# An attention kernel: rarer self-waits on ScalarE, a copy of K split over two queues, and the second Q's cast and the V loads held back

## The chip, the cores and the metric

The kernel runs on one core of a Trainium2 chip. The metric is the device time of one execution in microseconds (us), the median of several runs. The profile's span, from the first to the last instruction, is about 1.8 us shorter than that time; all times inside the kernel count from the start of the span.

## The reference

Grouped-query attention, 8 batches, 8 query heads, 2 key/value heads, 1024 tokens, head size 64, all float32 (cut):

```python
scores = scale * np.matmul(q_group, k_group.transpose(0, 1, 3, 2))
scores_max = np.max(scores, axis=-1, keepdims=True)
attn = np.exp(scores - scores_max)
attn = attn / (np.sum(attn, axis=-1, keepdims=True) + 1e-08)
output[:, q_start:q_end, :, :] = np.matmul(attn, v_group)
```

## The kernel before

A planner splits the work into 128 jobs (a batch, a head, one half of its queries) of 8 cells (128 keys x 512 queries), and decides for each cell whether ScalarE takes the exp, two cells to a tile, or VectorE with an approximation made of bits. It also sets the order on every engine. One constant tells it when the second half of the first K is there:

```python
FIRST_TURN, FIRST_LOAD, EACH_LOAD = 3.3, 4.5, 4.2
...
def loaded(j):
    h = j // 2
    if not h:
        return FIRST_TURN * (j % 2)
```

ScalarE writes its exps into a ring of 28 tiles. Every eighth tile waits for a result of ScalarE itself, so that the following ones need not:

```python
exp_ins.append(act.ins)
if n >= P_TILES and n % OBSERVE == 0:          # OBSERVE = 8, P_TILES = 28
    seen = exp_ins[n - P_TILES + OBSERVE - 1]
    tc.add_manual_dep(act.ins, seen.name, SYNC, reason="ring")
```

The first head has no time for DMA transposes: K and Q are loaded in halves, cast, and turned (transposed) by TensorE into PSUM, the memory that TensorE writes; TensorE is kept busy with matmuls on a blank tile (`keep_warm`). Jobs of side 0 use K on partitions 0 to 63 (`lo`), jobs of side 1 use it on 64 to 127 (`hi`). The `hi` half is a copy of the `lo` half by one DMA from GpSimd (cut; the comments are mine):

```python
cast(("q", 0, 1), q[0, 1])            # head 1's Q, GpSimd, issued at once
for two in range(2):
    place_v(0, 0, two)                # V, GpSimd
...
last_score[0] = keep_warm(WARM)       # 30 blank matmuls
...                                   # halves of K and Q: cast, turn, copy from PSUM
nc.scalar.copy(out=qT[(0, 0)][:, : HALF // 2], in_=tq[0][:, : HALF // 2])
turn_k(1, slice(0, NHC), 0)
last_score[0] = keep_warm(4)
put_k(0, 1, slice(0, NHC), 0)
nc.gpsimd.dma_start(out=ksets[0][hi, 0, 1, :], in_=ksets[0][lo, 0, 0, :])
```

The softmax here doesn't subtract the row's maximum and nothing guards it: scores larger than these inputs give would overflow.

## Time and profile before

| | before |
|---|---|
| time, median of 3 runs | 386.83 us (386.65 to 386.90) |
| span of the profiled run | 384.9 us |
| exp tiles on ScalarE | 406, one every 0.917 us |
| first, fourth exp start | 6.47, 9.80 us |
| end of the 403rd exp to end of span | 8.34 us |

From the page of the kernel before, first the busy times (us, share of the span, instructions), then the chain of work that ended last (share by engine):

```profile
PE 368.1 (96%) x5172; PEld 234.5 (61%) x5172; DVE 350.1 (91%) x544; ACT 375.1 (97%) x411; POOL 165.3 (43%) x147
```

```profile
ACT 94%; PE 2%; DMA 1%; issue 1%; DVE 0%; SPq 0%; POOLq 0%
```

TensorE and ScalarE are both nearly always busy. The chain tells which of them sets the end: ScalarE, for 94% of the span. The other 6% of 384.9 us, some 23 us, lie at the start and the end, so a change that doesn't touch ScalarE's rate can only earn there.

### The profile page before, as it was taken

Reading aid. Unit: us, or ns where it says so; the run is one execution under the profiler, and the core shown is the slowest. Engines: PE = TensorE matmul, PEld = TensorE weight load, DVE = VectorE, ACT = ScalarE, POOL = GpSimd, SP = SyncE. Lnnn points to the kernel's source line nnn. Section 1 sums busy time; section 2 is a strip of 40 time slices with the busy share of each in tenths; the row PEclk is TensorE's granted clock in tenths of the full one; section 3 lists DMA queues with packets and bytes.
Section 4 is the critical chain, followed back from the end, with each engine's and each line's share of the span. In section 5 each row is a group of like instructions: output and inputs, shape, how many; then the busy total and the mean of one; then the engine's idle time right before and its main releaser. Section 6 shows DMA issues by size and latency. Waiting matters only on the chain.

```text
span 384.9 us, 12057 instructions
## 1 busy us (share of the span) xinstructions
PE 368.1 (96%) x5172; PEld 234.5 (61%) x5172; DVE 350.1 (91%) x544; ACT 375.1 (97%) x411; POOL 165.3 (43%) x147
## 2 busy tenths in 40 slices
PE   8879999999999999999999999999999999999985
PEld 6425565656666666666666565666566566666654
DVE  4879999999999999999999999999999999999692
ACT  5999999999999999999999999999999999999994
POOL 5394571716246171625535252535445261531410
PEclk9999999999999999999999999999999999999998
DMA  8888979597859769595865949486584756621213
GB/s 137 152 130 141 141 138 173 113 129 148 128 111 134 132 109 141 123 138 85 151 123 126 125 90 169 74 150 113 119 143 109 111 100 113 109 70 29 71 43 83
DMA packets 102422, 45.49 MB, mean 118 GB/s; under 512 B 63776, under 2 KB 100896, under 8 KB 101120
## 3 DMA queue, kind: packets, MB, share of 16 engines
q1 hardware_dynamic: 82096, 31.21, 37.5%
q0 software_dynamic: 19728, 13.25, 29.8%
q8 instruction: 40, 0.66, 0.8%
q10 hardware_dynamic: 544, 0.26, 0.2%
q14 instruction: 14, 0.11, 0.1%
HBM read 25.17 MB, written 27.00 MB: 136 GB/s over the span
## 4 chain that ended last, share of the span: by engine, by line
ACT 94%; PE 2%; DMA 1%; issue 1%; DVE 0%; SPq 0%; POOLq 0%
ACT p_ring L463 94%; PE ops L522 1%; PE aps L452 1%; DMA fk<-in_k_dram 1%; DMA kset<-kset 1%; SPq L389 0%; DVE ost L538 0%; ACT hk L411 0%; DVE kset L382 0%; DVE qT L427 0%; PE aps L373 0%; DVE rec L535 0%; PE ops L419 0%; PE ops L400 0%; POOLq L433 0%
## 5 line engine op out<-in xcount | busy, mean ns | idle before, releaser
L463 ACT ACTIVATE p_ring<-aps 128x1024 bf16<-128x1024 f32 x406 | 372.4, 1100 | 1.2 <-PE aps L452 1.2
L452 PE MATMUL aps<-qT,kset 128*128 128x512 bf16 x812 | 240.6, 378 | 11.4 <-ACT p_ring L463 8.8
L522 PEld LDWEIGHTS <-p_ring 128*128 128x128 bf16 x3248 | 137.5, 97 | 60.4 <-ACT p_ring L463 0.2
L522 PE MATMUL ops<-vset,p_ring 128*128 128x65 bf16 x3248 | 150.8, 194 | 0.1
L477 DVE TENSOR_SCALAR pd<-dps 128x512 uint16<-128x512 f32 x212 | 138.0, 682 | 13.2 <-PE dps L452 12.3
L500 POOL TENSOR_SCALAR y<-z 128x5120 f16<-128x5120 uint16 (+1 forms) x22 | 94.6, 4301 | 82.7 <-DVE rec L535 45.0
L452 PEld LDWEIGHTS <-kset 128*128 128x128 bf16 x1024 | 82.6, 97 | 58.8 <-issue 26.7
L314 POOL DMA_DIRECT2D scr_q<-in_q_dram x63 | 34.7, 551 | 99.0 <-PE aps L452 47.6
L452 PE MATMUL dps<-qT,kset 128*128 128x512 bf16 x212 | 73.4, 378 | 0.0
L511 DVE TENSOR_TENSOR pd<-pd,y 128x5120 uint16<-128x5120 uint16 (+1 forms) x22 | 59.8, 2719 | 0.1
L509 DVE TENSOR_TENSOR y<-z,y 128x5120 f16<-128x5120 uint16 (+1 forms) x22 | 59.8, 2718 | 0.0
L538 DVE TENSOR_TENSOR ost<-ops,rec 128x256 f32<-128x256 f32 x128 | 54.3, 424 | 4.4
L522 PEld LDWEIGHTS <-pd 128*128 128x128 bf16 x848 | 41.3, 98 | 25.6 <-DVE pd L511 3.6
L522 PE MATMUL ops<-vset,pd 128*128 128x65 bf16 x848 | 48.4, 194 | 0.0
L496 DVE TENSOR_SCALAR z<-pd 128x5120 uint16<-128x5120 uint16 (+1 forms) x22 | 31.7, 1443 | 0.6
L535 DVE RECIPROCAL rec<-ops 128x4 f32<-128x4 f32 x128 | 22.5, 176 | 9.8 <-PE ops L522 8.8
L347 POOL DMA_DIRECT2D vset<-in_v_dram x32 | 24.9, 782 | 0.0
L314 POOL DMA_DIRECT2D scr_k<-in_k_dram x15 | 7.8, 521 | 24.1 <-PE aps L452 16.7
L400 PE MATMUL ops<-blank 128*128 128x128 bf16 x40 | 4.4, 286 | 1.1 <-DVE blank L279 1.1
L400 PEld LDWEIGHTS <-blank 128*128 128x128 bf16 x40 | 3.8, 135 | 1.1 <-DVE blank L279 1.1
L354 POOL DMA_DIRECT2D kset<-kset x6 | 3.2, 537 | 0.0
L411 ACT ACT_TABLE_LOAD x1 | 1.3, 1283 | 1.8 <-issue 1.8
(23 smaller groups left out, 8.7 us busy)
## 6 DMA issues: line engine op xcount, KB each, us to landing
out_dram<-ost SPq DMA_DIRECT2D x63, 256.0 KB, 2.9
scr_q<-in_q_dram POOLq DMA_DIRECT2D x63, 128.0 KB, 3.6
kset<-kT SPq DMA_DIRECT2D x60, 64.0 KB, 3.1
vset<-in_v_dram POOLq DMA_DIRECT2D x32, 64.0 KB, 4.0
scr_k<-in_k_dram POOLq DMA_DIRECT2D x15, 128.0 KB, 3.2
qT<-scr_q SPq DMA_TRANSPOSE x63, 4.0
kset<-kset POOLq DMA_DIRECT2D x7, 128.0 KB, 4.0
fq<-in_q_dram ACTq DMA_DIRECT2D x2, 128.0 KB, 3.2
```

The costliest lines, as they stand in the source:

```text
L314: dma = nc.gpsimd.dma_start(out=scr.rearrange("(p f) -> p f", f=1024), in_=src.rearrange("(p s) d -> p (s d)", s=1024 // D),)
L347: nc.gpsimd.dma_start(out=vsets[b % 2][:, g, two * NHC : (two + 1) * NHC, 0:D], in_=v[b, g].rearrange("(c p two) d -> two p c d", p=128, t ...
L452: last_score[0] = nc.tensor.matmul(dst, lhsT=ksets[b % 2][:, h // HPG, side, c * 128 : (c + 1) * 128], rhs=qT[(b, h)], start=True, stop=Tr ...
L463: act = nc.scalar.activation(out=pt[:, 0:m], in_=psum.pop(("A", n))[:, 0:m], func=AF.Exp, scale=scale)
L477: nc.vector.tensor_scalar(out=groups[g][:, slot], in0=psum.pop(cell), scalar1=bits_scale, scalar2=bits_bias, op0=ALU.mult, op1=ALU.add,)
L496: eng.tensor_scalar(out=z, in0=pd, scalar1=0x7F, scalar2=None, op0=ALU.bitwise_and)
L500: eng.tensor_scalar(out=y, in0=z, scalar1=CURVE_A / 128.0, scalar2=CURVE_B, op0=ALU.mult, op1=ALU.add,)
L509: eng.tensor_tensor(out=y, in0=z, in1=y, op=ALU.mult)
L511: eng.tensor_tensor(out=pd, in0=pd, in1=y, op=ALU.add)
L522: nc.tensor.matmul(ops_of[s][:, qs, :], lhsT=p_of[cell][:, qs * 128 : (qs + 1) * 128], rhs=vsets[b % 2][:, h // HPG, c, :], start=opens an ...
L535: nc.vector.reciprocal(out=rec, in_=o[:, :, D])
L538: nc.vector.tensor_tensor(out=stage[(b, h)][:, :, side, :], in0=o[:, :, 0:D], in1=rec.unsqueeze(2).to_broadcast([128, NQS, D]), op=ALU.mult,)
```

## The change

It has three parts, and a constant that goes with them. The self-wait comes once in 26 tiles. The copy of K to `hi` becomes two DMAs: the even keys from ScalarE, as soon as its own copy is done, the odd keys from GpSimd as before. The cast of the second Q and the V loads wait for the 14th blank matmul, to leave the DMA engines to the first K and Q. The planner is told that the copy comes earlier (2.4 instead of 3.3).

```diff
-    FIRST_TURN, FIRST_LOAD, EACH_LOAD = 3.3, 4.5, 4.2
+    FIRST_TURN, FIRST_LOAD, EACH_LOAD = 2.4, 4.5, 4.2
...
-    OBSERVE = 8
+    OBSERVE = 26
...
-        cast(("q", 0, 1), q[0, 1])
-        for two in range(2):
-            place_v(0, 0, two)
...
-        last_score[0] = keep_warm(WARM)
+        last_score[0] = keep_warm(14)
+        cast(("q", 0, 1), q[0, 1])
+        for two in range(2):
+            place_v(0, 0, two)
+        last_score[0] = keep_warm(WARM - 14)
...
+        nc.scalar.dma_start(
+            out=ksets[0][hi, 0, 1, :HALF], in_=ksets[0][lo, 0, 0, :HALF]
+        )
...
-        nc.gpsimd.dma_start(out=ksets[0][hi, 0, 1, :], in_=ksets[0][lo, 0, 0, :])
+        nc.gpsimd.dma_start(
+            out=ksets[0][hi, 0, 1, HALF:], in_=ksets[0][lo, 0, 0, HALF:]
+        )
...
-        if n >= P_TILES and n % OBSERVE == 0:
+        if n >= P_TILES and (n - P_TILES) % OBSERVE == 0:
```

## The prediction

> **What bounds the kernel now.** I read the page first (busy time, groups), then the chain of work in order of time, then the windows view of ScalarE's exp tiles, then the timeline of both ends.
>
> The groups of the page give the work of ScalarE: 406 exp tiles, and next to no idle time ahead of them (1.2 us in all, TensorE being awaited).
>
> ```profile
> L463 ACT ACTIVATE p_ring<-aps 128x1024 bf16<-128x1024 f32 x406 | 372.4, 1100 | 1.2 <-PE aps L452 1.2
> ```
>
> The chain in order of time shows the beginning, and how the first self-wait looks (start us, length us, what):
>
> ```profile
> 1.26 3.09 DMA fk<-in_k_dram
> 4.35 0.02 issue
> 4.37 0.41 ACT hk L411
> ...
> 5.38 0.29 DVE qT L427
> 5.67 0.36 DVE kset L382
> 6.03 0.02 issue
> 6.05 0.02 POOLq L433
> 6.07 0.56 issue
> 6.63 2.48 DMA kset<-kset
> 9.11 0.05 issue
> 9.15 0.62 PE aps L452 x2
> 9.77 0.02 issue
> 9.80 22.80 ACT p_ring L463 x25
> 32.60 0.05 issue
> 32.65 0.87 ACT p_ring L463
> ```
>
> One chain leads from the K load over casts and transposes to the copy of K to the second partition half; this copy lands at 9.11, and the fourth exp starts at 9.80 because of it. From there on the chain is ScalarE alone. The "issue" piece at 32.60 is the first self-wait; after the first five such pieces come, in the same view, one for every 8 tiles, each of 0.04 to 0.09 us. A reader would now multiply: 51 self-waits before (counted in the built program), some 0.05 us each, 2 to 3 us. The windows view says otherwise (stretch, busy, tiles that touch it):
>
> ```profile
> 10.82:32.82 22.00, 22.00 (x25) 1.00 0.83 137
> 33.74:374.75 341.01, 341.01 (x373) 1.00 0.68 117
> ```
>
> I put the edges on ends of tiles (the timeline gives the starts and durations: 9.80 + 1.02 is the end of the fourth exp, 32.65 + 1.09 that of the first one with a self-wait). One tile in each count only reaches over the right edge, so there are 24 and 372 ends. 22.00 / 24 = 0.917 us without a self-wait, 341.01 / 372 = 0.917 us with one in every 8. Tiles last 1.02 to 1.15 us and overlap; a waiting tile starts later and lasts less, its end comes when it would have come. So ScalarE's own rate, 0.917 us a tile, bounds the program from 9.8 to about 377, and the self-waits hide in the overlap.
>
> The timeline of the end (columns: start, length, engine, line, operation):
>
> ```profile
> 376.38 2.95 ACT L463 ACTIVATE p_ring<-aps 128x1024 bf16<-128x1024 f32 x3
> ...
> 377.55 0.59 PE L452 MATMUL aps<-qT,kset 128*128 128x512 bf16 x2
> ...
> 379.82 0.90 PE L522 MATMUL ops<-vset,p_ring 128*128 128x65 bf16 x24
> ```
>
> The last exp ends at 376.38 + 2.95 = 379.33, but TensorE still works on its backlog of output matmuls until 380.72, then come the last division and the store. The last score matmul (377.55) starts as the exp two tiles before the last ends, one free PSUM tile being what it needs.
>
> **What the Trainium skill says.** "ScalarE: Activation LUTs", section "What ACT_TABLE_LOAD costs": 186 ns + 0.833 ns an element for an ACTIVATE with immediate scale, overlapping the next one by some 93 ns; for 1024 elements 1039 - 93 = 946 ns. The trace has tiles of 1100 ns mean every 917 ns, so more overlap than the page states; 917 = 853 + 64 I take from the trace. "Perfetto Trace Analysis", section "Per-instruction lifecycle": for this engine the window starts when execution starts, and the semaphore wait in the wait queue is outside of it. This fits: a wait shows only as a later start, and costs only if the end moves. "DMA: Bandwidth & Descriptors", section "Latency and other measured facts": first byte some 0.6 us on the hardware path, 1 us on the software path. The trace agrees in direction: the software copy of K took 2.48 us from issue to landing (128 KB, a lone transfer), and copies of 64 KB into the same tile from SyncE have medians of 2.3 us (window 60 to 90 us) to 3.1 us (whole page). Same page, "Issuing engines are not separate DMA queues": all share 16 engines, so what ScalarE's issue gains is time of issue, not bandwidth.
>
> **The change part by part.**
>
> *Self-waits.* The built programs have 51 ACTIVATEs with a self-wait before and 15 after. 36 are removed; at the rate above each was worth 0, sum 0. The new wait looks back to the exp 3 before instead of 21 before. That one ended about 3 x 0.917 - 1.10 = 1.65 us before the new tile's start, so it should be satisfied too: cost 0.
>
> *K copy.* Before, exps 1 to 3 start at 6.47 and run 2.85 us, ending at 9.32; the fourth ends at 10.82 instead of 9.32 + 0.92 = 10.24. The stall is 0.58 us, and no more than this can be had. After: the even half is issued by ScalarE when its copy into the tile is done (the program waits for its third result, 5.15 + 0.37 = 5.52, and for an older result of VectorE), so at about 5.6, landing 2.3 to 3.1 us later: 7.9 to 8.7. The planner's constant (3.3 to 2.4) now puts two cells of output matmuls, one VectorE score, then the fourth tile's two scores there. To keep the rate this exp must start by 10.24 - 1.02 = 9.22, so the three scores (3 x 0.216 issue, plus 0.4 for the last to finish) must start by about 8.3. Landing is before that in the lower two thirds of the interval, so I take 0.1 us of the 0.58 as remaining: gain 0.48. The issue takes ScalarE's sequencer some 0.5 us, 5.6 to 6.1, while the first exp waits for scores until 6.43: hidden. The odd half, on GpSimd, waits for VectorE only (done 6.02), as before, is half as large, and must be there at 9.3, when the fifth tile's PSUM comes free: hidden.
>
> *First Q cast and V loads.* They now wait for the 14th warm-up matmul (ends about 2.73) instead of being issued at 1.34. But before, the first packets of the cast only started at 3.61 us, and on each DMA engine behind the last packets of the K and Q loads; these are done at 3.9 (K) and 4.2 (Q). There is little to relieve: I take 0.05 us of gain. On the other side V lands at about 3.4 + 3.4 = 6.8, needed at 8.0, and the cast at about 6.2, with its transpose (3.8 us in the trace) at 10.1, needed at about 10.7: both hidden, the second barely.
>
> *What the plan moves.* 1024 cells were 812 for ScalarE (406 tiles) and 212 for VectorE; now 813 and 211, the 407th exp being half a tile, worth 0.427 + 0.064 = 0.49 us of ScalarE if it bounded the end. It doesn't quite. Counted from the end of the exp whose PSUM the before's last scores took: before, 2 scores and 21 cells of 4 output matmuls, 2 x 0.216 + 21 x 0.124 = 3.04 us. After, the single last score waits for one more tile, then 17 cells: 0.917 + 0.216 + 17 x 0.124 = 3.24 us. Loss 0.20.
>
> Sum: 386.83 - 0.48 - 0.05 + 0.20 + 0 = **386.5 us**.
>
> **The rivals.**
> *The self-waits do cost.* The pieces in the chain speak for it: 36 x 0.05 to 0.07 is 1.8 to 2.5 us, time 384.0 to 384.7. Against it are the two rates of 0.917. If TensorE's loop (end of exp, two scores, start of the exp after next) and not ScalarE set that rate, removing the waits would still give nothing. Chance 4%.
> *A DMA takes the place of the one removed.* The hardware copy at its median of 3.1 us under load, beside the V loads that now fall at the same time, or V and the head's Q arriving late: the fourth exp waits as before, and only the added half tile stays: 386.9 to 387.1. For it: the cast and V traffic moved exactly to 5 to 7 us. Against it: a copy of 64 KB has little to move. Chance 25%.
> *ScalarE's DMA issue delays the first exp.* If the issue starts 0.5 us late, as the GpSimd copy did at 6.07 to 6.63, it ends at 6.6 and everything shifts by 0.2: 386.7. Chance 15%.
> *A new order elsewhere.* The plan of all 128 jobs is recomputed, so a late Q or K could stop ScalarE once, by 0.5 us or more. In the kernel before, no tile of the last 402 ended more than 0.02 us late; chance 10%.
>
> **Range and chances.** The sum's own doubts are some 0.3 us either way, the runs of before spread over 0.25 us. Range 386.0 to 387.0. Two per cent are 7.7 us, more than anything in reach: faster 0.01, same 0.98, slower 0.01.
>
> **What would show it.** Right: exp ends 0.917 us apart in the windows view over the whole middle; fourth exp ending at 10.2 to 10.4; 407 exps; TensorE finishing about 0.2 us later counted from the fourth exp. Wrong: a mean spacing of 0.912 or less (self-waits did cost), the fourth exp still at 9.8, a first exp later than 6.5, or idle time ahead of an exp in the middle.

## The result, and the profile after

The changed kernel took 387.32 us (387.24 to 387.65, 4 runs), the kernel before 386.87 us (386.65 to 387.09, 4 runs); the ratio is 1.0013, 95% interval 0.9996 to 1.0031. Within 2% it is the same, but not the small gain predicted: 387.32 lies above the range of 386.0 to 387.0.

The group of exp tiles on the changed kernel's page:

```profile
L469 ACT ACTIVATE p_ring<-aps 128x1024 bf16<-128x1024 f32 (+1 forms) x407 | 372.9, 1110 | 1.1 <-PE aps L458 1.1
```

The windows view of the same tiles (stretch, busy, tiles that touch it), edges again on ends of tiles:

```profile
34.00:376.83 342.83, 342.83 (x374) 1.00 0.66 117
```

There are 407 tiles, and 374 ends in 342.83 us: 0.917 us each, as before, with 15 self-waits instead of 51. Nothing was won in the middle.

The chain of the changed kernel in order of time, its first 33 us (start, length, what):

```profile
1.06 3.38 PE ops L397 x30
...
6.36 0.43 PE ops L397 x4
...
7.29 25.58 ACT p_ring L469 x28
```

The K load and the copy of K are gone from the chain, and the fourth exp no longer stalls. But the first exp starts at 7.29 instead of 6.47 us, and the chain now leads through TensorE. Lines of both timelines (start, length, engine, line, operation) show why. The kernel before, near 4.2 us:

```profile
4.17 0.28 PE L373 MATMUL dps<-ident,hk 128*128 128x128 bf16 x2
4.28 0.28 PE L400 MATMUL ops<-blank 128*128 128x128 bf16 x2
```

The changed kernel at the same place:

```profile
4.23 0.42 PE L373 MATMUL dps<-ident,hk 128*128 128x128 bf16 x2
4.45 0.42 PE L397 MATMUL ops<-blank 128*128 128x128 bf16 x2
```

The same pairs of matmuls take half as long again, and start 0.22 instead of 0.11 us after each other: TensorE runs at half clock. The clock's records in the traces have it go to full speed ("the switch" from here on) at 4.08 us before and at 6.72 us after.

The copy of K didn't get faster. The DMA issues of the stretch from 5 to 9.5 us (DMA view; size, us from issue to landing) have, for the kernel before:

```profile
kset<-kset POOLq DMA_DIRECT2D x1, 128.0 KB, 2.5
```

For the even half in the changed kernel:

```profile
kset<-kset ACTq DMA_DIRECT2D x1, 64.0 KB, 3.2
```

Half as many bytes, issued by ScalarE at 5.94 us, landed at 9.16; the whole copy had landed at 9.11. The stall ahead of the fourth exp is small only because the three exps ahead of it were late themselves: it starts at 10.06 us, before it started at 9.80.

The timeline of the end of the changed kernel:

```profile
377.77 2.44 ACT L469 ACTIVATE p_ring<-aps 128x1024 bf16<-128x1024 f32 x3
...
378.86 0.38 PE L458 MATMUL aps<-qT,kset 128*128 128x512 bf16 x1
...
380.43 0.90 PE L528 MATMUL ops<-vset,p_ring 128*128 128x65 bf16 x24
```

The last exp, half a tile, ends at 380.20 instead of 379.33. In sum, from before to after: end of the fourth exp 10.82 to 11.08, +0.26; from there to the end of the 403rd 365.76 to 365.75, -0.01; from there to the end 8.34 to 8.64, +0.30. Together +0.55, which is the difference of the spans (384.92 and 385.47). The first of these terms compares two different clocks; the table below takes it up again.

### The profile page after: what moved, and what is told of

Its sections match the earlier page's. It is cut to its first block, busy times and chain, and to the rows that moved or that the text cites. A ratio compares the mean times of both kernels' runs of the same rounds, so it can differ in the third digit from the quotient of the medians.

```text
span 385.5 us, 11930 instructions
## 1 busy us (share of the span) xinstructions
PE 362.6 (94%) x5081; PEld 234.9 (61%) x5172; DVE 349.7 (91%) x543; ACT 375.6 (97%) x412; POOL 166.9 (43%) x147
## 4 chain that ended last, share of the span: by engine, by line
ACT 95%; PE 3%; issue 0%; DVE 0%
ACT p_ring L469 95%; PE ops L528 1%; PE ops L397 1%; PE aps L458 1%; PE dps L373 0%; DVE ost L544 0%; DVE rec L541 0%; PE dps L420 0%; PE ops L420 0%; PE aps L373 0%; DVE blank L279 0%
## 5 line engine op out<-in xcount | busy, mean ns | idle before, releaser
L469 ACT ACTIVATE p_ring<-aps 128x1024 bf16<-128x1024 f32 (+1 forms) x407 | 372.9, 1110 | 1.1 <-PE aps L458 1.1
L458 PE MATMUL aps<-qT,kset 128*128 128x512 bf16 x724 | 222.3, 378 | 12.9 <-ACT p_ring L469 10.8
L314 POOL DMA_DIRECT2D scr_q<-in_q_dram x63 | 36.0, 572 | 95.9 <-PE aps L458 47.8
L458 PE MATMUL dps<-qT,kset 128*128 128x512 bf16 x209 | 72.6, 378 | 1.8
L528 PEld LDWEIGHTS <-pd 128*128 128x128 bf16 x844 | 40.3, 97 | 23.8 <-DVE pd L517 2.4
L528 PE MATMUL ops<-vset,pd 128*128 128x65 bf16 x844 | 47.1, 194 | 0.7
L397 PE MATMUL ops<-blank 128*128 128x128 bf16 x40 | 5.3, 313 | 1.1 <-DVE blank L279 1.1
L354 POOL DMA_DIRECT2D kset<-kset x6 | 4.2, 706 | 0.0
```

Of the source, the lines that this page charges most:

```text
L314: dma = nc.gpsimd.dma_start(out=scr.rearrange("(p f) -> p f", f=1024), in_=src.rearrange("(p s) d -> p (s d)", s=1024 // D),)
L458: last_score[0] = nc.tensor.matmul(dst, lhsT=ksets[b % 2][:, h // HPG, side, c * 128 : (c + 1) * 128], rhs=qT[(b, h)], start=True, stop=Tr ...
L469: act = nc.scalar.activation(out=pt[:, 0:m], in_=psum.pop(("A", n))[:, 0:m], func=AF.Exp, scale=scale)
L528: nc.tensor.matmul(ops_of[s][:, qs, :], lhsT=p_of[cell][:, qs * 128 : (qs + 1) * 128], rhs=vsets[b % 2][:, h // HPG, c, :], start=opens an ...
```

## The experiments

Sixteen runs were made, in four groups; each group shares the runs of the kernel before. The times of the kernel before were 387.09, 387.18 and 386.88 us (medians of 9, 7 and 9 runs) in the first three groups; in the last one there is a single run of 386.85.

### Both kernels again: what scatters

The kernels are unchanged.

> The kernel before, unchanged, to see how much the start scatters. Theory A (the clock's switch to full speed comes on a grid of 3.4 us that runs free of the program): the matmul spacing changes from 107 to 56 ns at some time between 3.9 and 7.4 us that differs from execution to execution, and the first exp starts between 6.4 and 7.3 us accordingly; the five times spread over up to 0.8 us. Theory B (the switch belongs to the program, the change itself makes it late): the switch comes at about 4.1 us and the first exp at about 6.47 us again, times 386.7 to 387.1.

> The changed kernel, unchanged. Theory A: the switch of the clock is not at 6.7 us again save by chance; where it comes early, the first exp starts at 6.4 to 6.5 us and the fourth exp stalls by about 0.5 us (its K half lands some 3.2 us after the issue at about 5.6, so near 8.8). Theory B: switch at about 6.7 us and first exp at about 7.3 us again, times 387.2 to 387.7.

The kernel before took 387.08 us (386.79 to 387.23) against 387.09 for the other runs of itself, ratio 1.0. The clock's switch came at 3.76 us, the first exp at 6.46, the fourth at 9.87. The changed kernel took 387.33 us (387.08 to 387.46), ratio 1.0007 (0.9995 to 1.0020). Its switch came at 5.67 us this time, its first exp at 6.90. Its chain (start, length, what):

```profile
5.94 3.33 DMA kset<-kset
...
9.31 0.39 PE dps L458
9.70 0.45 PE aps L458 x2
...
10.17 2.85 ACT p_ring L469 x3
```

Now that ScalarE starts earlier, the copy of K is back in the chain, for 3.33 us. The fourth exp ends 1.44 us after the third instead of 0.92.

The switch follows theory A. It scattered from profile to profile, from 3.76 to 6.72 us. It goes on and off on one grid: 378.88 us apart in both first profiles, 382.29 in the repeat of before, which is 111 and 112 times 3.413 us; in e3 below it was on for 6.83 and then off for 3.41 us. The two profiles of the kernel before have it at 3.76 and 4.08, the six of the changed kernel at 5.16 to 6.72, so these alone can't exclude that the change makes it late. But the blank matmuls start at 1.06 us in both kernels, and the kernel before with nothing but the rarer self-waits (e10) has it at 6.10, with nothing but the split (e9) at 6.66. "TensorE: Matmul & The Clock Gate" in the Trainium skill, section "What's actually happening", says so: the window of 3413 ns is free-running and does not reset when a kernel starts. I had not used it. The table gives all profiles of the two kernels, and two of the others that leave the start of the kernel before alone:

| profile | switch | first exp | K to `hi`: issue, landing | fourth exp | 403rd exp's end to end of span |
|---|---|---|---|---|---|
| before | 4.08 | 6.47 | 6.63, 9.11 | 9.80 | 8.34 |
| before, repeated | 3.76 | 6.46 | 6.62, 9.18 | 9.87 | 8.32 |
| before, self-wait each | 4.49 | 6.86 | 7.02, 9.29 | 9.97 | 8.34 |
| before, self-wait rarer | 6.10 | 6.99 | 7.36, 9.63 | 10.32 | 8.33 |
| after | 6.72 | 7.29 | 5.94, 9.16 | 10.06 | 8.64 |
| after, repeated | 5.67 | 6.90 | 5.94, 9.27 | 10.17 | 8.62 |
| after, look a | 5.78 | 6.95 | 5.94, 9.21 | 10.12 | 8.63 |
| after, look b | 5.91 | 6.96 | 5.94, 9.41 | 10.31 | 8.63 |
| after, look c | 5.16 | 6.76 | 5.84, 8.80 | 9.71 | 8.63 |
| after, look d | 6.49 | 7.18 | 5.94, 8.98 | 9.91 | 8.62 |

In the changed kernel's rows the landing is that of the even half. (In the third row the second half of the K load landed 0.4 us later than in the others, so its first exp is late for its switch.) A switch that is 2.6 us later makes the first exp 0.8 us later, and whatever the first exp does, the fourth one starts 0.69 us after the landing before and 0.90 us after it in the changed kernel, where one more score of VectorE stands ahead. (Look d has 0.93, but there the fourth exp ended 0.916 us after the third and waited for nothing.)

The rows have to be compared at like clock. The kernel before is seen once with a late switch (self-wait rarer, 6.10): its copy landed at 9.63, its fourth exp started at 10.32 and ended at 11.34. In the five profiles of the changed kernel with the switch at 5.67 or later, the half landed at 8.98 to 9.41 and the fourth exp started at 9.91 to 10.31, at 10.11 in the mean. So with a late clock the fourth exp came some 0.2 us earlier, by five profiles against one; the +0.26 at its end in the first pair lies with the clock. With a switch as early as in the two profiles of the kernel before, the changed kernel was not seen.

### Holding back alone, and all but the holding back

```diff
# e3: the kernel before, with
-        cast(("q", 0, 1), q[0, 1]); place_v(0, 0, 0); place_v(0, 0, 1)   (ahead of the blank matmuls)
+        the same three behind keep_warm(14)
# e4: the changed kernel, with the three ahead of the blank matmuls again
```

> The kernel before, with only the first Q cast and the V loads held back behind 14 warm-up matmuls. Theory A: the K and Q loads land within 0.05 us of before (second halves at 4.35 and 4.63), the start depends on the clock's switch alone, and the copy of K by GpSimd, now beside the V loads, lands no earlier than 9.1 us; time within 0.3 us of before, rather above. Theory B: this is the part that makes the switch late: switch near 6.7 us, first exp near 7.3 us, time 387.2 or more. The intent of the change would be K and Q landing earlier by 0.2 us or more.

> The changed kernel without the holding back. If the held-back cast and V loads are what slows the K half's copy, it lands about 2.3 us after its issue instead of 3.2, the fourth exp stalls by less than 0.2 us, and the time is some 0.3 us below the changed kernel's at the same clock; if the copy is slow by itself, it lands after 3.2 us again and the time equals the changed kernel's. Theory B with the hold as cause: switch near 4.1 us again.

With the holding back alone the time was 387.70 us (387.40 to 389.72), ratio 1.0018 (1.0005 to 1.0032): it costs. The second halves of K and Q landed at 4.35 and 4.61 us, before at 4.35 and 4.64, so nothing was gained. Its profile shows the loss (chain):

```profile
6.74 4.21 DMA kset<-kset
```

The whole copy of K from GpSimd, issued at 6.74, took 4.21 us instead of 2.48. Beside it were now the second V load (landed at 7.53) and the third Q's cast (9.01, before 7.90); which of them slowed it no run separates. The fourth exp ended 3.76 us after the third, and in the gap the clock fell back to half from 10.59 to 14.00 us. This profiled run was the slowest of its six (389.72); the other five (387.40 to 388.25) show the usual size, and all of them lie above the highest run of the kernel before beside them (387.26).

The changed kernel without holding back took 387.13 us (386.51 to 387.52), ratio 1.0002 (0.9990 to 1.0015). V landed at 6.62 us instead of 7.73, but the even half of K only at 8.99, 3.08 us after its issue. So holding back alone is a loss, in the changed kernel its 0.2 us of median are not clear of the noise, and it isn't what makes ScalarE's copy slow: without it 3.08 us here and 3.29 in e9, with it 2.96 to 3.47.

### The self-waits

```diff
# e5: the kernel before, with
-    OBSERVE = 8
+    OBSERVE = 1
# e10: the kernel before, with the change's OBSERVE = 26 and (n - P_TILES) % OBSERVE == 0
```

> The kernel before with a self-wait on every exp tile from the 29th on: 378 instead of 51, nothing else moved. My reading (the wait lies in the overlap of two exps): ends stay 0.917 us apart, time as before within 0.3 us. The rival (each self-wait costs the 0.05 to 0.07 us of its gap in the chain): 327 more of them, plus 16 to 23 us, time 403 to 410 us.

> The kernel before with only the rarer self-wait (15 instead of 51, on the exp 3 before). Reading: ends stay 0.9167 us apart, time as before within 0.2 us. The author's intent, taken at the gaps in the chain: 36 x 0.05 to 0.07, so 1.8 to 2.5 us faster.

With 378 self-waits instead of 51 the time was 387.11 us (387.00 to 387.35) against 387.18, ratio 1.0003 (0.9988 to 1.0018). The windows view of the exp tiles:

```profile
33.91:377.04 343.13, 343.13 (x376) 1.00 0.69 117
```

374 ends (two of the tiles counted only touch the edges) in 343.13 us are 0.9175 us each instead of 0.9167. 327 more waits cost 0.3 us together, 1 ns each, not 50. With 15 self-waits alone the time was 387.20 us (386.81 to 387.33) against 386.88, ratio 1.0005 (0.9992 to 1.0019), with 342.87 us for 374 ends. All these waits were for exps long done (28, 21 or 3 tiles back), so they show what a wait costs that needn't wait. The first part of the change is worth nothing here, in both directions.

### The half tile at the end

```diff
# e6: the kernel before, with
-    FIRST_TURN, FIRST_LOAD, EACH_LOAD = 3.3, 4.5, 4.2
+    FIRST_TURN, FIRST_LOAD, EACH_LOAD = 3.4, 4.5, 4.2
```

> The kernel before with the planner's constant at 3.4 instead of 3.3: the first 14 scores keep their order, but ScalarE gets 813 cells instead of 812, so 407 tiles with half a tile last, as the changed kernel has. Reading: from the end of the 403rd exp to the end of the span 8.6 us instead of 8.34 (0.2 us of it predicted, 0.3 measured for the changed kernel), everything earlier as before; time some 0.3 us above before. Rival: the last half tile is hidden and the 0.3 us of the changed kernel came from elsewhere; then 8.34 us again.

From the end of the 403rd exp to the end it took 8.56 us instead of 8.32 to 8.34, so +0.22, my 0.20. The time, 387.11 us (386.91 to 387.65) against 387.18, ratio 1.0004 (0.9988 to 1.0021), is too coarse to show it. The changed kernel's other 0.08 us is in its own order: its 404th exp ends 1.03 us after the 403rd instead of 0.92, TensorE coming late with the scores, in each of its profiles and in all others with the constant 2.4.

### What slows ScalarE's copy

```diff
# e7: e4, and the first DMA transpose of Q also waits for the even copy of K
+        if key == ("q", 0, 1):
+            tc.add_manual_dep(turned.ins, even_copy[0].name, SYNC, reason="after K")
# e8: e4, with the even half on the other queue
-        nc.scalar.dma_start(out=ksets[0][hi, 0, 1, :HALF], ...)
+        nc.gpsimd.dma_start(out=ksets[0][hi, 0, 1, :HALF], ...)
```

> The changed kernel without the holding back, and with the first DMA transpose of Q on SyncE made to wait for the landing of the even K half. In the run without the holding back the half's first packets started at 7.46 us, just as the transpose's issue ended (7.45), though the DMA engines had been idle for 0.9 us. Reading 1 (the transpose's issue keeps the copy's packets back): the half lands 1.9 to 2.4 us after its issue, so at 7.6 to 8.4, and the fourth exp stalls by less than 0.2 us; the late Q may stall a later exp instead. Reading 2 (a copy from ScalarE needs 3.1 us in any case): lands at 8.7 to 9.1 us, stall as without the wait.

> The changed kernel without the holding back, with the even half issued by GpSimd too. Reading 1 (the delay sits in the hardware path that the transpose shares): issued at 5.9 to 6.5, it lands some 2.0 to 2.5 us later, at about 8.5, before the ScalarE copy of the other runs (9.0 to 9.27). Reading 2 (DMA engines are busy at that time): again at 9.0 or later.

With the transpose out of the way the half landed after 2.66 us instead of 3.08, and the fourth exp, started at 9.38 us, didn't stall (0.917 us after the third). But then the second head's Q came late (chain):

```profile
5.73 2.66 DMA kset<-kset
...
8.47 5.23 DMA qT<-scr_q
```

The seventh exp ended 3.59 us after the sixth, and the time was 388.92 us (388.43 to 391.07), ratio 1.0059 (1.0029 to 1.0090). So the transpose may be part of the delay, 0.4 us of it with one profile each; both readings were too simple. Even in this run the first packets came 1.42 us after the issue (1.55 in e4, 1.67 to 1.94 in the six profiles of the changed kernel). The packet records have nearly the same for ScalarE's very first DMA, the load of Q: issued at 0.74, first packets at 2.20 in the kernel before, and 1.43 to 1.68 us after the issue in all profiles, with only the first loads under way. So most of the 1.4 us need not be delay by other traffic: this queue has it on its first issue too. (Nor had the DMA engines been idle in e4, as the expectation has it: the DMA view books a packet where it starts, and sixteen packets of 8 KB, started at 6.00 to 6.32, were under way until 7.00 to 7.30.)

From GpSimd the half was issued at 6.20 and landed at 9.70 us, after 3.50 us: later still, against reading 1. Time 387.26 us (387.09 to 387.87), ratio 1.0009 (0.9994 to 1.0023).

### The split alone

```diff
# e9: the kernel before, with only the two nc.*.dma_start of the change; FIRST_TURN = 3.3, OBSERVE = 8, nothing held back
```

> The kernel before with the K copy split in two and nothing else: even half over ScalarE, odd half over GpSimd, planner's constant 3.3, so 406 tiles, casts where they were. Reading 1 (the half lands hardly earlier than the whole did): even half at 8.8 to 9.0 us instead of 9.1 to 9.2, the fourth exp's end 1.3 to 1.5 us after the third's, time within 0.2 us of before. Reading 2 (the split works, only the plan's half tile and the held-back cast spoil it): fourth end after 0.92 to 1.2 us, time 0.3 to 0.5 us below before.

386.93 us (386.80 to 387.20) against 386.88, ratio 1.0001 (0.9987 to 1.0014). With the switch at 6.66 us the even half landed at 9.23, and the fourth exp ended 1.05 us after the third and started at 10.14 us. Its chain (start, length, what; window 0 to 11.5):

```profile
9.25 0.42 PE ops L527 x8
9.67 0.45 PE aps L457 x2
...
10.14 1.94 ACT p_ring L468 x2
```

Here the fourth exp waited for output matmuls that the old plan puts ahead of its scores (as in e12 below, also 1.05), no longer for the copy. So the step is that of reading 2, helped by the late clock, which had delayed the first exp to 7.26; the time is that of reading 1. Splitting by itself earns nothing that the times of these runs can show.

### No DMA for K at all

TensorE's transposes put the even keys, and the odd keys, onto partitions 64 to 127 of PSUM anyway. Copying them from there by an engine needs no DMA:

```diff
# e11 (FIRST_TURN = 2.4) and e12 (FIRST_TURN = 3.3): the kernel before, with
+        def copy_odd(n):
+            cols = slice(halves[n].start * 128, halves[n].stop * 128)
+            nc.scalar.copy(out=ksets[0][hi, 0, 1, HALF:][:, cols], in_=tk[n][hi, cols])
...     (copy_odd(0) behind the second cast of K, copy_odd(1) behind the copy into qT)
-        nc.gpsimd.dma_start(out=ksets[0][hi, 0, 1, :], in_=ksets[0][lo, 0, 0, :])
+        put_k(1, 0, slice(0, NHC), 0)
```

> The kernel before with the planner's constant 2.4 and no DMA for K's second partition half: VectorE copies the even half, ScalarE the odd half out of the PSUM tiles in which the transposes put them on those partitions anyway. If the landing of K alone stalls the fourth exp, no exp stalls: ends 0.917 us apart from the first, with the clock's switch at any time. End of span 8.6 us after the 403rd exp as in every kernel with this plan. Time: 0.58 to 0.66 less for the stall, 0.3 more for the half tile, so about 0.3 us below before. If another wait takes its place (Q of the second head, V), the fourth or a later exp stalls by as much.

> The same copies by VectorE and ScalarE with the planner's constant 3.3, so the 406 tiles and the end of before. The fourth exp's scores then stand behind four cells of output matmuls, the last two of which wait for the second exp: its end comes about 1.2 us after the third's instead of 1.5. End of span 8.33 us after the 403rd exp. Time 0.25 to 0.35 us below before, about that of the run with the new plan.

With the change's plan, no exp stalls at the start, as the chain shows:

```profile
7.24 6.52 ACT p_ring L472 x7
```

The fourth exp ends 0.917 us after the third. The end took 8.68 us, as in all kernels with this plan. Time 386.60 us (386.53 to 387.26) against 386.88, ratio 0.9997 (0.9984 to 1.0009). With the old plan the fourth exp ended 1.05 us after the third, waiting for output matmuls, and the end took 8.33 us; time 386.94 us (386.25 to 387.23), ratio 0.9999 (0.9986 to 1.0011). With the switch at 6.62 and 6.36 us these two profiles alone don't show that the stall came from the landing of K: at so late a first exp the changed kernel hardly stalled either (0.94 us in its first profile, 0.92 in look d). What shows it is the fixed step from landing to fourth exp in the table, and e7, where the half landed at 8.39 and, with the first exp at 6.65, nothing stalled. Neither version is shown to beat the kernel before: the scatter that the phase of the clock's switch brings (up to 0.8 us at the first exp) is larger than the gain.

### Four more looks at the changed kernel

> The changed kernel at another phase of the clock. If the copy's landing is to blame: with the switch before 4.5 us, the even half is issued at about 5.6, lands 3.1 to 3.3 us later at 8.7 to 8.9, and the fourth exp starts at 9.6 to 9.8, as before (9.80 and 9.87), not at 9.2 as predicted; with a late switch at 10.0 to 10.2. If the clock is to blame: with an early switch the fourth exp starts at 9.2 to 9.3. From the 403rd exp's end to the end 8.6 us either way.

> Second look, expected as the first: fourth exp at 9.6 to 9.8 us after an early switch if the copy is to blame, 9.2 to 9.3 if the clock is.

> Third look, expected as the first: fourth exp at 9.6 to 9.8 us after an early switch if the copy is to blame, 9.2 to 9.3 if the clock is.

> Fourth look, expected as the first: fourth exp at 9.6 to 9.8 us after an early switch if the copy is to blame, 9.2 to 9.3 if the clock is.

None fell on a switch before 4.5 us, so the start that I had predicted for was never seen in the changed kernel. The earliest, 5.16 us, has the half landing after 2.96 us at 8.80 and the fourth exp at 9.71, where before it was 9.80 with an earlier switch. The half's time from issue to landing in the six profiles is 2.96 to 3.47 us, mean 3.2. The times, single runs of unknown state, were 387.68, 387.48, 386.87 and 390.50 us. The first and the last show what else can come late. The chain of look a:

```profile
6.11 5.98 DMA qT<-scr_q
```

The chain of look d:

```profile
7.11 5.07 DMA kset<-kset
```

In look a the second head's Q, cast later and so transposed later (from 6.11; 5.53 in the kernel before), arrived at 12.09 us, and the seventh exp ended 0.34 us late. In look d the odd half of K needed 5.07 us; the fifth exp ended 2.0 us late, TensorE idled, and its clock fell to half from 13.32 to 16.73 us. Two more exps ended late, by 0.6 and 0.7 us.

## Why the prediction was wrong, point by point

**Bound and self-waits: right.** ScalarE's 0.917 us a tile is the rate of the middle, and the self-waits hide in the overlap. This was shown in both directions, down to 15 and up to 378.

**K copy: the step that failed.** It is the one that says "landing 2.3 to 3.1 us later: 7.9 to 8.7", "so I take 0.1 us of the 0.58 as remaining: gain 0.48". The durations were taken from copies in the middle of the kernel. At the start the copy lies beside the V loads, the casts and the Q transpose and needed 3.0 to 3.5 us in the changed kernel; half the bytes were no faster than the whole (2.3 to 2.6 us from GpSimd in the four profiles of the table that have it). It was issued at 5.84 to 5.94, not at about 5.6, because the clock was late in all six profiles; that is 0.7 to 1.5 us earlier than the whole copy, and it lost most of that on the way: landing at 8.80 to 9.41 against 9.11 to 9.63, and the fourth exp at 9.71 to 10.31 against 9.80 to 10.32. The gain is not 0.48 us but some 0.2 at a late clock, by few profiles, and unseen at an early one. Two of the prediction's own signs of being wrong came: a first exp later than 6.5, and a fourth that starts at 9.71 at best, about where it was before.

The prediction could have seen some of this. It says that the trace agrees in direction with a faster hardware path, but its own lines have 2.48 us for 128 KB from GpSimd and 2.3 to 3.1 us for 64 KB from SyncE. Nor was that copy a lone transfer: the transpose of Q, issued at 5.53, landed at 9.29. Its sum "3 x 0.216 issue, plus 0.4" leads from 9.22 to 8.2, not 8.3 (0.90 us was measured from landing to exp, so 8.3 is right), and of its interval the lower half, not two thirds, lies before 8.3. And the odd half, "hidden" if there at 9.3, landed at 9.63 to 10.40, in look d at 12.18.

My second rival, "a DMA takes the place of the one removed", held at 25%, is what came, with 386.9 to 387.1 us for it.

**The clock: a term that was missing.** I took TensorE's start as fixed. It scatters by 0.8 us with the phase of a free-running window. This moves both kernels, so it explains little of the difference between them. But I started from 386.83, the median of three runs, and put the range at "the runs of before spread over 0.25 us"; 31 more runs of the kernel before, its repeat among them, spread from 386.65 to 387.48, over 0.83 us. With 386.83 the terms that were measured give 386.9 to 387.1, at the edge of the range; the rest lies within this scatter. That the first profile of the changed kernel had the latest switch of all I take for chance.

**ScalarE's DMA issue delays the first exp: not seen.** The issue took 0.54 us at 5.94, and the first exp waited for scores until 7.26, at the late clock. In e7, with a switch at 4.94 us, it ended at 6.24, the exp started at 6.65.

**Holding back: wrong in sign.** 0.05 us of gain was put down, and V and Q judged hidden, "the second barely". The loads landed at the same time within 0.04 us (first profiles and e3). What was held back then met the copy of K in the one profile of it: holding back alone cost 0.6 us of median time, and once (look a) Q was the wait.

**Half tile at the end: mechanism right, size off.** 0.20 us predicted, 0.22 by itself in e6, 0.28 to 0.31 in the changed kernel, because its own order makes TensorE late for the 404th exp.

In sum, in place of -0.48 - 0.05 + 0.20 the runs show -0.2 to 0 for the start and +0.3 for the end; at 387.09 us for before this gives 387.2 to 387.4, and 387.33 was measured beside it. What stays open: what stretches the copy beyond the 1.4 us of its issue, the transpose having been taken out in one profile alone, and what the changed kernel does when the switch is early.

## What to carry to other kernels

Ask whether the ends of the bounding engine's instructions move, not whether there are gaps between pieces of its chain: a wait inside the overlap of two instructions was free here. A transfer at the start of a kernel takes what it takes beside the others in flight there, so take its duration from that place, and count each further transfer as one more that can be late; where the data already lies in PSUM on the right partitions, a copy by an engine takes that landing out of the chain (e11, e12). And before predicting differences below 0.2%, look at how the kernel scatters by itself, and compare profiles only at like clock.

## What the Trainium skill lacked or had wrong

- "ScalarE: Activation LUTs": it has back-to-back ACTIVATEs overlapping by some 93 ns; here exps of 1024 elements came every 917 ns at a mean of 1100 ns each, an overlap of 183 ns. (The prediction's 946 ns is an estimate from figures there that are for immediate scale and bias; whether these exps have an immediate bias no run shows.)
- No page that I found says that a self-wait in a stream of ACTIVATEs is free where it is already fulfilled: 327 more of them cost 1 ns each; such tiles last 1079 ns in the median (e5, 36 to 100 us), those without a wait 1149 (before, 10.83 to 32.82 us), and the ends stay 917 ns apart.
- "TensorE: Matmul & The Clock Gate" has the free-running window of 3413 ns right (111 and 112 times it between on and off). It tells not to fit to a count of slow matmuls and puts the penalty under 1% of a span. That holds here, but the scatter of the first exp alone, 0.8 us or 0.2%, is more than the change under study.
- "DMA: Bandwidth & Descriptors": it gives the hardware path 0.6 us to the first byte. Here the first load from SyncE needed 1.10 to 1.13 us from issue to the first packet, the first one from ScalarE 1.43 to 1.68 (all profiles), and ScalarE's copy of 64 KB 1.67 in the first profile of the changed kernel, and 2.96 to 3.47 us to landing, more than the software path's 2.3 to 2.6 for twice the bytes.
